# Gate and up products of a Strassen-style feed-forward: the second product of the next weight matrix moved between the third and fourth of the current one

## Chip, core and metric

The kernel runs on one core of one Trainium2 chip. The metric is device time in microseconds (us) for one execution; a version's time is the median of its runs. One execution per version is also recorded by the hardware profiler, with its own time; the trace comes from that execution.

## The reference

A two-layer encoder on a sequence of 1024 rows of width 1024. Layer 0 mixes with FNet and convolution heads, layer 1 with pooling; the change touches neither. Each layer ends with a feed-forward block, whose inner width is 2816, and the change is in the first half of it:

```python
def swiglu_ffn(h, w_gate, w_up, w_down):
    return (jax.nn.silu(h @ w_gate) * (h @ w_up)) @ w_down

for layer in range(DEPTH):
    ...
    h = rmsnorm(x, norm_ffn_g[layer])
    x = x + swiglu_ffn(h, ffn_w_gate[layer], ffn_w_up[layer], ffn_w_down[layer])
```

## The kernel before, in words

Everything is float32. TensorE gets each operand as a high part and a low remainder (`split`, lines 87 to 89: ScalarE casts, VectorE subtracts), and `mm3` (lines 99 to 104) multiplies in three matmuls: high by high (L101), high by low (L102), low by high (L103). In traces every product therefore has the lines L101 to L103, whoever calls it.

**The unit of work.** The 22 blocks of 128 columns of the gate matrix, and of the up matrix, are taken in pairs, 11 a layer. A pair of blocks of one matrix is multiplied with the two halves of the sequence in a Strassen-Winograd scheme of seven products. One product (`product`, lines 553 to 557) is 4 times 3 = 12 matmuls of 128x128 by 128x512. Two of the seven, A11 B11 and A12 B21, are made for all pairs by `gate_up_first` (lines 608 to 624), which also writes the first to memory (`p1_dram`). The other five are made later, in `gate_up_all` (lines 719 to 737), for one matrix of one pair at a time: here called a unit. A layer has 22 units, alternately gate (`up` false) and up (`up` true); gate units end with a silu on ScalarE, up units with a multiplication on VectorE and a store.

**What a unit needs** is set up by `prep` (lines 626 to 644): the saved first product is loaded into an SBUF tile `p1` and copied by ScalarE into a PSUM bank, the seed (L629, L630); two raw weight tiles of 512 KB are loaded (L595); VectorE forms the differences and sums (L635 to L637, L642), and each of five left operands S2, S1, S3, A22, S4 is cast and split (L88, L89).

**What a unit does** (`gate_up_rest`, lines 690 to 710), in the order of the program: product S2 T2 is added onto the seed (L696, "second product"); ScalarE copies the result into the bank `bd` and into the SBUF tile `u2` (L697, L698); S1 T1 goes into the bank `bc` (L699); S3 T3 is added onto `bd` (L700, "third product"); ScalarE copies `bd` to the SBUF tile `x` (L701), VectorE adds `bc` and `x` (L703); then A22 T4 is added onto the same bank `bd` (L705, "fourth product"), which must wait until L701 has read it; S4 B22 is added onto `bc` (L707), and L709 adds `u2`. `fin` (lines 646 to 652) finishes each of the three outputs (L649 silu, L651 multiplication and store).

**Buffers.** PSUM has eight banks: four under the tag "ps", two under "lnp", two under "acc". Seeds come from "ps"; `bc` and `bd` from "ps" in gate units and from "lnp" in up units (`banks2`, L603 to L606). Tiles `p1`, `s3` and `u2` share one tag of four SBUF buffers ("ln", `small`, L58); split weights share ten ("w": five operands of two units, high and low part side by side in one tile), raw weights three. In the profile's names `p` is `p1`, `s` is `s3`, and `u` is `u2`.

**What sets the order.** The loop writes prep of unit u+1 ahead of the products of unit u. A planner in the framework then orders every engine's queue ahead of time by its own estimate of durations: an instruction whose inputs and buffers are there in the estimate is placed, and of several the one that stands earlier in the program. Buffers of a tag are handed out in the program's order. On the chip each queue then runs strictly in that planned order, each instruction waiting on semaphores for what it needs. Weight and `p1` loads are issued from SyncE's queue (SPq), stores from GpSimd's (POOL). In layer 1 `left_sums` (L675 to L688) and `right_sums` (L664 to L673) add loads, VectorE sums and stores per pair for the down projection.

Of the kernel before, what the change touches and what calls it, by code (L numbers as in the profile page):

```python
# [42 lines left out]
def trunk(ctx: ExitStack, tc: tile.TileContext, xT, vecs, cw, w_in, w_out, fmap, pmap,  # L43
          wg, wu, wd, wdq, wdp, cen_m, pcnt, dft_h, dft_l, seq_h, seq_l, out):
    nc = tc.nc
# [9 lines left out]
    def half(name, dt=F32):  # L55
        return arena.tile([P, TH], dt, tag="half", name=name, bufs=HALF_BUFS)

    def small(name, dt=F32):  # L58
        return arena.tile([P, TH], dt, tag="ln", name=name, bufs=4)

    def bank(tag="ps"):
        return psum.tile([P, TH], F32, tag=tag, name=tag, bufs=4 if tag == "ps" else 2)
# [36 lines left out]
    def mm3(ps, lhs, rhs, start, stop, **kw):  # L99
        (lh, ll), (rh, rl) = lhs, rhs  # L100
        nc.tensor.matmul(ps, lh, rh, start=start, stop=False, **kw)  # L101
        nc.tensor.matmul(ps, lh, rl, start=False, stop=False, **kw)  # L102
        mm = nc.tensor.matmul(ps, ll, rh, start=False, stop=stop, **kw)  # L103
        marks.append((marks[-1][0] + 3 * ps.free_size(), mm))
# [85 lines left out]
    def in_w(m, **kw):  # L190
        return load_w(w_in[m], **kw)
# [207 lines left out]
    def pool_w(*args):  # L399
        behind["at"] = max(behind["at"], marks[-1][0]) + 5500  # L400
        return load_w(*args, eng=nc.gpsimd)
# [20 lines left out]
    for h in range(4):  # L422
        w = in_w(h)
# [25 lines left out]
    def fnet1(cp, h):  # L449
        wcs = []  # L450
        for c in (2 * cp, 2 * cp + 1):
            ps = bank()
            psv = ps.rearrange("p (j n) -> p j n", j=2)
            for j in range(2):
                n = len(PLAN[c])
                for i, (zi, tb) in enumerate(PLAN[c]):
                    o = zi * 256 + j * P
                    rhs = tuple(tt[h // 2][:, h % 2, tb:tb + 2, :].rearrange("p a e -> p (a e)")
                                for tt in (tb_h, tb_l))
                    mm3(psv[:, j, :], (z_h[h][:, o:o + P], z_l[h][:, o:o + P]), rhs, i == 0, i == n - 1)  # L460
            wh, wl = half("wch", F32R), half("wcl", F32R)
            nc.scalar.copy(wh, ps)
            TT(out=wl, in0=ps, in1=wh.bitcast(F32), op=ALU.subtract)
            wcs.append((wh, wl))
        return wcs
# [22 lines left out]
    for i, (cp, h) in enumerate(steps):  # L488
        nxt = fnet1(*steps[i + 1]) if i + 1 < len(steps) else None
# [16 lines left out]
    for mp in range(4):  # L506
        w = pool_w(w_out[mp])
# [40 lines left out]
    def opnd(src, alloc):  # L548
        t = alloc("hl", dt=F32R)
        split(t[:, :TH], t[:, TH:], src)  # L550
        return t

    def product(ps, w, b, start, stop):
        for j in range(4):
            c = j * P
            mm3(ps, (w[:, c:c + P], w[:, TH + c:TH + c + P]), (b[j][:, :TH], b[j][:, TH:]),
                start and j == 0, stop and j == 3, skip_group_check=not start)
# [35 lines left out]
    def raw_w(src):  # L593
        raw = arena.tile([P, 1024], F32, tag="raw", name="raw", bufs=3)
        nc.sync.dma_start(raw, src)  # L595
        return raw[:, :TH], raw[:, TH:]
# [3 lines left out]

    nbank = [0]

    def banks2():  # L603
        nbank[0] += 1
        tag = "ps" if nbank[0] % 2 else "lnp"
        return bank(tag), bank(tag)  # L606

    def gate_up_first(layer, p, bt):

        g = half("g11")  # L610
        for i, wsrc in enumerate((wg, wu)):
            a11, a12 = raw_w(wsrc[layer, 2 * p])
            a11, a12 = opnd(a11, wt), opnd(a12, wt)
            ps = bank(("lnp", "ps")[i])
            product(ps, a11, bt["B11"], True, True)
            s1 = half("s1")
            nc.scalar.copy(s1, ps)
            nc.gpsimd.dma_start(p1_dram[layer][p][i], s1)
            product(ps, a12, bt["B21"], False, True)
            if i == 0:  # L620
                nc.scalar.activation(g, ps, AF.Silu)
            else:
                TT(out=g, in0=ps, in1=g, op=ALU.mult)
        store_b(layer, "B11", p, g)

    def prep(layer, p, wsrc):

        p1, bb = small("p1"), bank()
        nc.sync.dma_start(p1, p1_dram[layer][p][int(wsrc is wu)])  # L629
        nc.scalar.copy(bb, p1)  # L630
        a11, a12 = raw_w(wsrc[layer, 2 * p])
        a21, a22 = raw_w(wsrc[layer, 2 * p + 1])
        w = {"seed": bb}
        s3 = small("s3")
        TT(out=s3, in0=a11, in1=a21, op=ALU.subtract)  # L635
        TT(out=a21, in0=a21, in1=a22, op=ALU.add)
        TT(out=a11, in0=a21, in1=a11, op=ALU.subtract)  # L637
        w["S2"] = opnd(a11, wt)
        w["S1"] = opnd(a21, wt)
        w["S3"] = opnd(s3, wt)  # L640
        w["A22"] = opnd(a22, wt)
        TT(out=a12, in0=a12, in1=a11, op=ALU.subtract)  # L642
        w["S4"] = opnd(a12, wt)
        return w

    def fin(layer, up, dst, src, m, t, tmp=None):

        if not up:
            nc.scalar.activation(dst, src, AF.Silu)  # L649
        else:  # L650
            TT(out=dst, in0=src, in1=dst, op=ALU.mult)  # L651
            store_b(layer, "B%d%d" % (m % 2 + 1, t + 1), m // 2, dst)

    def store_b(layer, name, p, src):
        if layer == 0:
            m, t = 2 * p + int(name[1]) - 1, int(name[2]) - 1
            nc.gpsimd.dma_start(a_dram[0][m][:, HALVES[t]], src)
        elif name != "B12":
            nc.gpsimd.dma_start(b_dram[name][p], src)
# [15 lines left out]
    def left_sums(p):  # L675


        q = [half("q") for _ in range(4)]
        for i in range(4):
            nc.sync.dma_start(q[i], wdq[p, :, i, :])  # L680
        a11, a12, a21, a22 = q
        TT(out=a22, in0=a21, in1=a22, op=ALU.add)
        TT(out=a21, in0=a11, in1=a21, op=ALU.subtract)
        TT(out=a11, in0=a22, in1=a11, op=ALU.subtract)
        TT(out=a12, in0=a12, in1=a11, op=ALU.subtract)
        for name, src in (("S3", a21), ("S2", a11), ("S1", a22), ("S4", a12)):
            nc.gpsimd.dma_start(s_dram[name].rearrange("r (j p c) -> r p j c", j=4, c=P)[:, p],  # L687
                                src.rearrange("r (j c) -> r j c", j=4))  # L688

    def gate_up_rest(layer, p, bt, w, up, g):  # L690


        bb, bc, bd = w["seed"], *banks2()
        m1, m2 = 2 * p, 2 * p + 1
        u2, x = small("u2"), half("x")
        product(bb, w["S2"], bt["T2"], False, True)  # L696
        nc.scalar.copy(bd, bb)  # L697
        nc.scalar.copy(u2, bb)  # L698
        product(bc, w["S1"], bt["T1"], True, True)  # L699
        product(bd, w["S3"], bt["T3"], False, True)  # L700
        nc.scalar.copy(x, bd)  # L701
        c22 = x if up else g["22"]
        TT(out=c22, in0=bc, in1=x, op=ALU.add)  # L703
        fin(layer, up, g["22"], c22, m2, 1)
        product(bd, w["A22"], bt["T4"], False, True)  # L705
        fin(layer, up, g["21"], bd, m2, 0)
        product(bc, w["S4"], bt["B22"], False, True)  # L707
        c12 = u2 if up else g["12"]
        TT(out=c12, in0=bc, in1=u2, op=ALU.add)  # L709
        fin(layer, up, g["12"], c12, m1, 1)  # L710
# [3 lines left out]
    def load_right(name, p):  # L714
        raw = half("rawb") if name == "B11" else spare(("cv", "pr")[p % 2])
        nc.sync.dma_start(raw, b_dram[name][p])
        return opnd(raw, big)

    def gate_up_all(layer, bt):
        seq = [(p, up) for p in range(NF // 2) for up in (False, True)]  # L720
        w = prep(layer, 0, wg)
        g = None
        for i, (p, up) in enumerate(seq):
            nxt = None
            if i + 1 < len(seq):
                q, qup = seq[i + 1]
                nxt = prep(layer, q, wu if qup else wg)
            if not up:
                g = {k: arena.tile([P, TH], F32, tag="cvp", name=f"g{k}", bufs=4) for k in ("22", "21", "12")}
            if layer == 1 and not up:  # L730
                left_sums(p)
            gate_up_rest(layer, p, bt, w, up, g)
            if layer == 1 and up:
                right_sums(p, g)
                if p >= NF // 2 - 4:
                    first_right.extend([load_right("B11", len(first_right) + r) for r in range(2)])
            w = nxt

    def new_b():
        return {k: [] for k in ("B11", "B21", "B22", "T1", "T2", "T3", "T4")}  # L740
# [141 lines left out]
    bt, hf = new_b(), []  # L882
# [91 lines left out]


    gate_up_all(1, b1)

    def out_of(lo, hi, inv):
# [117 lines left out]
```

## Time and profile before

| What | Value |
|---|---|
| Median of three runs | 1733.5 us (1731.33 to 1737.66) |
| The profiled execution | 1727.4 us, of which the trace spans 1725.6 us |
| Mean granted TensorE clock | 0.991 |
| TensorE matmuls busy | 1656.9 us, 96% of the span |
| VectorE, ScalarE, GpSimd busy | 1215.0, 793.9, 349.4 us |
| Chain that ended last | 71% TensorE, 11% VectorE, 8% issue, 6% DMA |
| The 22 units of layer 0, from the first to the last L697 | 465.4 to 760.9 us |
| The 22 units of layer 1, likewise | 1179.7 to 1487.4 us |

"Busy" counts an engine as busy while any of its instructions is open. A matmul row lasts some 0.39 us, but the next one starts about 0.23 us after it, so rows overlap, and their sum is more than the busy time. Some matmul records, a few per cent, are missing from a trace. A bracket at the end of a timeline row tells how long that engine had been idle, and whose end released it.

### The profile page before, as it was taken

Reading aid. Unit: us, or ns where it says so; the run is one execution under the profiler, and the core shown is the slowest. Engines: PE = TensorE matmul, PEld = TensorE weight load, DVE = VectorE, ACT = ScalarE, POOL = GpSimd, SP = SyncE. Lnnn points to the kernel's source line nnn. Section 1 sums busy time; section 2 is a strip of 40 time slices with the busy share of each in tenths; the row PEclk is TensorE's granted clock in tenths of the full one; section 3 lists DMA queues with packets and bytes.
Section 4 is the critical chain, followed back from the end, with each engine's and each line's share of the span. In section 5 each row is a group of like instructions: output and inputs, shape, how many; then the busy total and the mean of one; then the engine's idle time right before and its main releaser. Section 6 shows DMA issues by size and latency. Waiting matters only on the chain.

```text
span 1725.6 us, 21770 instructions
## 1 busy us (share of the span) xinstructions
PE 1656.9 (96%) x7790; PEld 1353.6 (78%) x7790; DVE 1215.0 (70%) x1727; ACT 793.9 (46%) x1283; POOL 349.4 (20%) x400
## 2 busy tenths in 40 slices
PE   6998789999999999999999998999999999999997
PEld 4786777777787787779998886777777778888877
DVE  8699997785455656555558877787767677656666
ACT  5555756474444444433334335454343435354443
POOL 4486764211100000000000001211212121204000
PEclk9999899999999999999999999999999999999999
DMA  5121311445633333346443434655767677886664
GB/s 188 49 98 38 126 70 37 165 165 195 243 113 127 116 124 129 120 131 195 132 137 103 155 102 145 216 176 195 232 220 237 209 239 255 278 276 189 201 194 131
DMA packets 101517, 278.23 MB, mean 161 GB/s; under 512 B 13088, under 2 KB 18464, under 8 KB 101408
## 3 DMA queue, kind: packets, MB, share of 16 engines
q1 hardware_dynamic: 77760, 203.16, 36.5%
q0 software_dynamic: 21344, 70.53, 11.7%
q10 hardware_dynamic: 2304, 3.15, 0.5%
q8 instruction: 61, 1.00, 0.2%
q14 instruction: 48, 0.39, 0.1%
HBM read 209.42 MB, written 67.37 MB: 160 GB/s over the span
## 4 chain that ended last, share of the span: by engine, by line
PE 71%; DVE 11%; issue 8%; DMA 6%; ACT 2%; POOL 1%; SPq 0%; POOLq 0%; DVEq 0%; ACTq 0%
PE ps L101 16%; PE ps L103 16%; PE ps L102 16%; PE lnp L101 7%; PE lnp L103 7%; PE lnp L102 7%; DMA p<-p 3%; DVE acc L315 2%; DVE acc L135 1%; DVE hl L89 1%; DMA xin<-in_xT 1%; DMA bT<-cv 1%; ACT x L701 1%; POOL sS L687 0%; ACT hl L88 0%
## 5 line engine op out<-in xcount | busy, mean ns | idle before, releaser
L101 PE MATMUL ps<-hl 128*128 128x512 f32 x704 | 274.9, 396 | 11.2 <-ACT x L701 8.3
L102 PE MATMUL ps<-hl 128*128 128x512 f32 x704 | 276.6, 393 | 0.0
L103 PE MATMUL ps<-hl 128*128 128x512 f32 x704 | 273.5, 394 | 0.0
L88 ACT CAST hl<-raw 128x512 fp32r<-128x512 f32 x264 | 159.7, 619 | 243.8 <-PE lnp L103 96.3
L89 DVE TENSOR_TENSOR hl<-raw,hl 128x512 fp32r<-128x512 f32 x264 | 179.0, 689 | 118.4 <-ACT hl L88 118.2
L88 ACT CAST wh<-raw 128x1024 fp32r<-128x1024 f32 (+4 forms) x147 | 127.9, 870 | 198.8 <-PE ps L102 88.2
L101 PE MATMUL lnp<-hl 128*128 128x512 f32 x528 | 211.7, 401 | 6.1 <-ACT x L701 5.1
L103 PE MATMUL lnp<-hl 128*128 128x512 f32 x528 | 208.2, 395 | 0.0
L102 PE MATMUL lnp<-hl 128*128 128x512 f32 x528 | 208.0, 394 | 0.0
L89 DVE TENSOR_TENSOR wl<-raw,wh 128x896 fp32r<-128x896 f32 (+4 forms) x135 | 136.3, 1012 | 61.0 <-ACT wh L88 50.3
L101 PEld LDWEIGHTS ps<-hl 128*128 128x128 f32 x704 | 132.2, 188 | 51.3 <-ACT x L701 15.2
L103 PEld LDWEIGHTS ps<-hl 128*128 128x128 f32 x704 | 132.2, 188 | 30.5
L102 PEld LDWEIGHTS ps<-hl 128*128 128x128 f32 x704 | 132.3, 188 | 29.1
L305 POOL TENSOR_TENSOR cvp<-cvp,pr 128x512 f32<-128x512 f32 x96 | 137.6, 1434 | 84.6 <-ACT pr L304 80.3
L101 PEld LDWEIGHTS lnp<-hl 128*128 128x128 f32 x528 | 99.5, 188 | 38.7 <-ACT x L701 12.5
L103 PEld LDWEIGHTS lnp<-hl 128*128 128x128 f32 x528 | 99.5, 188 | 23.0
L102 PEld LDWEIGHTS lnp<-hl 128*128 128x128 f32 x528 | 99.6, 189 | 22.2 <-issue 0.7
L101 PE MATMUL ps<-ahl,wh 128*128 128x504 f32 (+2 forms) x358 | 115.3, 322 | 0.0
L103 PE MATMUL ps<-ahl,wl 128*128 128x504 f32 (+2 forms) x358 | 114.8, 321 | 0.0
L102 PE MATMUL ps<-ahl,wh 128*128 128x504 f32 (+2 forms) x358 | 114.7, 320 | 0.0
L101 PE MATMUL ps<-hl,wh 128*128 128x512 f32 (+1 forms) x308 | 111.8, 363 | 0.0
L103 PE MATMUL ps<-hl,wl 128*128 128x512 f32 (+1 forms) x308 | 111.4, 362 | 0.0
(242 smaller groups left out, 3410.9 us busy)
## 6 DMA issues: line engine op xcount, KB each, us to landing
raw<-in_wg SPq DMA_DIRECT2D x66, 512.0 KB, 4.0
raw<-in_wu SPq DMA_DIRECT2D x66, 512.0 KB, 3.8
raw<-in_wd SPq DMA_DIRECT2D x32, 448.0 KB, 3.4
p<-s POOLq DMA_DIRECT2D x44, 256.0 KB, 3.1
p<-p SPq DMA_DIRECT2D x44, 256.0 KB, 4.7
a<-g POOLq DMA_DIRECT2D x44, 256.0 KB, 2.8
q<-in_wdq SPq DMA_DIRECT2D x44, 256.0 KB, 6.2
sS<-q POOLq DMA_DIRECT2D x44, 256.0 KB, 4.6
```

Of the source, the lines that this page charges most:

```text
L88: nc.scalar.copy(hi, src)
L89: (eng or nc.vector).tensor_tensor(out=lo, in0=src, in1=hi.bitcast(F32), op=ALU.subtract)
L101: nc.tensor.matmul(ps, lh, rh, start=start, stop=False, **kw)
L102: nc.tensor.matmul(ps, lh, rl, start=False, stop=False, **kw)
L103: mm = nc.tensor.matmul(ps, ll, rh, start=False, stop=stop, **kw)
L135: TT(out=acc, in0=acc, in1=sq, op=ALU.add)
L305: nc.gpsimd.tensor_tensor(out=a, in0=a, in1=pr, op=ALU.add)
L315: STT(out=acc, in0=src, scalar=wv, in1=acc, op0=ALU.mult, op1=ALU.add)
L701: nc.scalar.copy(x, bd)
```

## The change

`second` is a new function that holds what opened `gate_up_rest`: it takes the bank `bd` and the tile `u2`, multiplies S2 by T2 onto the seed and makes the two copies. It is called for the first unit of a layer right after that unit's `prep`, so ahead of the second unit's `prep`. For each later unit it is called through `between()` inside the products of the unit before it: behind the third product's copy, sum and `fin`, and ahead of the fourth product. In the last unit of a layer `between()` does nothing. The program's order of products thus goes from S2, S1, S3, A22, S4 of one unit to S1, S3 of this unit, S2 of the next, A22, S4 of this one. The number of instructions of each kind is the same. The bank `bd` and the tile `u2` are asked for, and filled, two products earlier relative to their own unit's S1 than before, and the order in which the four "ln" buffers are asked for changes from p1, s3 of unit u+2 after u2 of unit u to p1, s3 of unit u+2 after u2 of unit u+1. The tag of the banks alternates as before.

```diff
-    def banks2():
-        nbank[0] += 1
-        tag = "ps" if nbank[0] % 2 else "lnp"
-        return bank(tag), bank(tag)
...
-    def gate_up_rest(layer, p, bt, w, up, g):
-
-
-        bb, bc, bd = w["seed"], *banks2()
+    def second(bt, w):
+
+        nbank[0] += 1
+        w["tag"] = "ps" if nbank[0] % 2 else "lnp"
+        w["bd"], w["u2"] = bank(w["tag"]), small("u2")
+        product(w["seed"], w["S2"], bt["T2"], False, True)
+        nc.scalar.copy(w["bd"], w["seed"])
+        nc.scalar.copy(w["u2"], w["seed"])
+
+    def gate_up_rest(layer, p, bt, w, up, g, between):
+
+
+
+        bd, u2, bc = w["bd"], w["u2"], bank(w["tag"])
         m1, m2 = 2 * p, 2 * p + 1
-        u2, x = small("u2"), half("x")
-        product(bb, w["S2"], bt["T2"], False, True)
-        nc.scalar.copy(bd, bb)
-        nc.scalar.copy(u2, bb)
+        x = half("x")
         product(bc, w["S1"], bt["T1"], True, True)
         product(bd, w["S3"], bt["T3"], False, True)
         nc.scalar.copy(x, bd)
         c22 = x if up else g["22"]
         TT(out=c22, in0=bc, in1=x, op=ALU.add)
         fin(layer, up, g["22"], c22, m2, 1)
+        between()
         product(bd, w["A22"], bt["T4"], False, True)
         fin(layer, up, g["21"], bd, m2, 0)
         product(bc, w["S4"], bt["B22"], False, True)
...
         w = prep(layer, 0, wg)
+        second(bt, w)
         g = None
...
-            gate_up_rest(layer, p, bt, w, up, g)
+            gate_up_rest(layer, p, bt, w, up, g, lambda: nxt and second(bt, nxt))
```

## The prediction

> **What bounds the kernel now.** I read the page first: share of each engine, then the costliest groups with the idle time before them.
>
> ```profile
> span 1725.6 us, 21770 instructions
> ...
> PE 1656.9 (96%) x7790; PEld 1353.6 (78%) x7790; DVE 1215.0 (70%) x1727; ACT 793.9 (46%) x1283; POOL 349.4 (20%) x400
> ...
> L101 PE MATMUL ps<-hl 128*128 128x512 f32 x704 | 274.9, 396 | 11.2 <-ACT x L701 8.3
> ...
> L101 PE MATMUL lnp<-hl 128*128 128x512 f32 x528 | 211.7, 401 | 6.1 <-ACT x L701 5.1
> ```
>
> TensorE is the bound, and of the 17.3 us for which it stands idle before these two groups, 13.4 us end with L701, the copy of `bd` into `x` that the fourth product waits for. That is the wait that the change puts other work into. The waits of PE by stage, first for layer 1's units and then for layer 0's (columns: total us, times, longest), say where they lie:
>
> ```profile
> PE ps L101 <- ACT x L701: 7.7, 7, 1.5
> PE lnp L101 <- ACT x L701: 3.9, 3, 2.4
> ```
>
> ```profile
> PE lnp L101 <- ACT x L701: 1.3, 1, 1.3
> PE ps L101 <- ACT x L701: 0.6, 3, 0.2
> ```
>
> Layer 1 has 11.6 us of them, layer 0 only 1.9 us. Why so little, at one wait per unit? The timeline of an up unit in layer 0 shows it:
>
> ```profile
> 569.48 0.40 PE L103 MATMUL lnp<-hl 128*128 128x512 f32 x1
> 569.71 0.40 PE L102 MATMUL ps<-hl 128*128 128x512 f32 x1
> ...
> 570.25 0.58 ACT L701 COPY x<-lnp 128x512 f32<-128x512 f32 x1
> ...
> 570.41 0.40 PE L102 MATMUL ps<-hl 128*128 128x512 f32 x1
> ...
> 570.88 0.50 PE L101 MATMUL lnp<-hl 128*128 128x512 f32 x1
> ```
>
> The last matmul of the third product starts at 569.48, the fourth product at 570.88, and between them run matmuls into a "ps" bank. In an up unit only the next unit's seed is in "ps": the planner has already put four matmuls of the next second product (569.71 to 570.41) into the wait, as many as its estimate of the copy holds. The program's new order asks for all twelve. In layer 1 four are not enough:
>
> ```profile
> 1212.39 0.76 SPq L629 DMA_DIRECT2D p<-p  x1
> ...
> 1218.63 0.59 ACT L630 COPY ps<-p 128x512 f32<-128x512 f32 x1 [5.76 <-DMA p<-p]
> 1219.15 0.58 ACT L701 COPY x<-ps 128x512 f32<-128x512 f32 x1
> ...
> 1219.78 0.50 PE L101 MATMUL ps<-hl 128*128 128x512 f32 x1 [1.37 <-ACT x L701]
> ```
>
> On ScalarE's queue the copy to `x` stands behind the copy of a later unit's seed, L630, which waited 5.76 us for its load; `x` follows it by 0.52 us, and TensorE loses 1.37 us.
>
> **The removed wait, from both sides.** From below: the rows of waits sum to 11.6 + 1.9 = 13.5 us. One of them stays, since the last unit of layer 0 has no next second product:
>
> ```profile
> 767.45 0.50 PE L101 MATMUL lnp<-hl 128*128 128x512 f32 x1 [1.25 <-ACT x L701]
> ```
>
> 13.5 - 1.25 = 12.2 us can go. Do they go wholly? The cover grows by eight matmuls. Their spacing comes from two rows fifteen matmuls apart, with no gap between:
>
> ```profile
> 572.37 0.40 PE L101 MATMUL lnp<-hl 128*128 128x512 f32 x1
> ...
> 575.83 0.40 PE L101 MATMUL lnp<-hl 128*128 128x512 f32 x1
> ```
>
> (575.83 - 572.37)/15 = 0.2307 us. A product is 12 x 0.2307 = 2.77 us, a unit 60 x 0.2307 = 13.84 us, and eight matmuls 1.85 us. Of all waits only the longest, 2.4 us, exceeds 1.85, by 0.5. So they go, even if `x` still stands behind a late seed; the 0.5 goes into the bound.
>
> From above: TensorE's whole loss in the stage, by the period of the units. L697 ends each unit's second product; here are the up units of layer 0, then of layer 1 (eleven each, first and last start):
>
> ```profile
> L697 ACT COPY lnp<-ps x11: 570/570/577, 479.8 to 760.9; 128x512 f32<-128x512 f32 x11
> ```
>
> ```profile
> L697 ACT COPY lnp<-ps x11: 570/570/579, 1195.6 to 1487.4; 128x512 f32<-128x512 f32 x11
> ```
>
> (760.9 - 479.8)/20 = 14.06 us and (1487.4 - 1195.6)/20 = 14.59 us a unit, 0.22 and 0.75 us over 13.84. With 21 units per layer that have a follower: 21 x 0.97 = 20.3 us. Some of the difference of 8 us is this, behind the longest wait:
>
> ```profile
> 1202.75 0.50 PE L101 MATMUL lnp<-hl 128*128 128x512 f32 x1 [2.37 <-ACT x L701]
> ...
> 1203.67 0.63 PE L101 MATMUL lnp<-hl 128*128 128x512 f32 x1
> ...
> 1206.66 0.47 PE L102 MATMUL lnp<-hl 128*128 128x512 f32 x1
> ```
>
> Seven spacings take 2.99 us, 0.43 each, where 7 x 0.2307 = 1.61: after 2.37 us of idling TensorE ran at nearly half speed and lost 1.4 us more. No other wait is followed by this; I count it with the wait that goes: 12.2 + 1.4 = 13.6 us. I stay at this end, as it is made of single rows.
>
> The Trainium skill, "TensorE: Matmul & The Clock Gate", section "What's actually happening", has the clock fall to half after an idle window of about 3.4 us. By that rule a 2.37 us wait costs no speed, and the sum would be 1.4 us smaller; the row shows the fall after a shorter gap, and I go by the row.
>
> **What moves, and what covers it.** The copies `bd` and `u2` of the next unit move with the second product; they are wanted by S3 three products later, 8.3 us, and take some 0.6 us each. At the border of two units S4 is now followed by S1 into a bank that nobody has used for a unit. No instruction is added; POOL's stores keep their place.
>
> The critical thing is what feeds the moved product, the four "ln" buffers. Now the load of `p1` is issued about when `u2` is first written, and the rest of the preparation follows:
>
> ```profile
> 564.31 0.36 SPq L629 DMA_DIRECT2D p<-p  x1
> ...
> 564.60 0.59 ACT L698 COPY u<-ps 128x512 f32<-128x512 f32 x1
> ...
> 565.20 0.69 DVE L635 TENSOR_TENSOR s<-raw 128x512 f32<-128x512 f32 x1 [1.36 <-DMA raw<-in_wu]
> ...
> 568.03 0.69 DVE L89 TENSOR_TENSOR hl<-raw,hl 128x512 fp32r<-128x512 f32 x1
> ```
>
> After the change `p1` and `s3` of unit u+2 come behind `u2` of unit u+1 in the order of hand-out. So their load and L635 can begin when the second product of unit u+1 ends, and the second product of u+2 is wanted four products later: 48 x 0.2307 = 11.07 us (before: nine products, 24.9 us). The weights take 568.03 + 0.69 - 565.20 = 3.5 us from L635 to the split S2. The seed takes 0.3 us to the issue (as far apart as the first two rows are), the landing, and 0.6 us for the copy; landing of `p`, layer 1 and then layer 0 (min/median/max):
>
> ```profile
> DMA to landing us min/median/max: 2.3/5.0/8.6
> ```
>
> ```profile
> DMA to landing us min/median/max: 3.1/4.6/5.3
> ```
>
> Even 8.6 us gives 9.5, inside 11.07. In the steady state I cost the move at nothing; the cover left is 5.2 us at the median, and if it is gone, every us more stops TensorE for one.
>
> At the entry it costs something. Before, the second unit's preparation began ahead of the first unit's second product, in layer 1 at 1176.92 against an end at 1179.66:
>
> ```profile
> 1176.92 0.69 DVE L635 TENSOR_TENSOR s<-raw 128x512 f32<-128x512 f32 x1 [1.02 <-DMA raw<-in_wu]
> ...
> 1179.66 0.57 ACT L697 COPY ps<-ps 128x512 f32<-128x512 f32 x1 [4.49 <-PE ps L103]
> ```
>
> Now it follows it, and the product is wanted only S1 and S3 later, 24 x 0.2307 = 5.5 us. The seed needs 0.3 + 5.0 + 0.6 = 5.9 us in layer 1 and 5.5 in layer 0: 0.4 us lost at the medians, 4.0 at 8.6. I take 0.8 us for both layers, between 0 and 4.
>
> **Sum.** 13.6 - 0.8 = 12.8 us gained; bounds 12.2 - 0.5 - 4 = 7.7 and 20.3. The profiled execution of 1727.4 us would take 1714.6. It lies 6.1 us under the median of 1733.5, which would become 1720.7.
>
> **Rivals.** *The next second product is late (slower).* TensorE runs matmuls in order, so if `p1` or S2 is late, A22 and S4 stand behind it though they are ready. This decides if the buffer handed to `p1` is that of the current unit's `u2`, as strict rotation of four would have it: it is free only after the unit's last use of it. S4's end starts L709 (576.73 below); in an up unit L651 then reads `u2` until 577.99 + 0.69, 1.95 us after; in a gate unit L709 is the last, 0.69 us. Then 1.3 on average + 5.0 + 0.6 = 6.9 us against 5.5: 1.4 us a unit in layer 1, 1.0 in layer 0, 21 x 2.4 = 50 us, less the 12.8: 1733.5 + 37 = 1771. It bites from a landing of 3.6 us on. Against it, by rotation this `p1` would now wait for that same `u2`:
>
> ```profile
> 576.73 0.69 DVE L709 TENSOR_TENSOR u<-lnp,u 128x512 f32<-128x512 f32 x1 [1.43 <-PE lnp L103]
> ...
> 577.99 0.69 DVE L651 TENSOR_TENSOR g<-u,g 128x512 f32<-128x512 f32 x1
> ...
> 578.54 0.37 SPq L629 DMA_DIRECT2D p<-p  x1
> ```
>
> The load starts 0.14 us before L651 ends, so it got another buffer. For it: the hand-out may change with the order. 0.14.
>
> The Trainium skill, same page, section "Step-by-step: what each phase is for", says that matmuls stay in program order. The trace agrees: in the 2.37 us at 1202.75 the rest of the second product, whose inputs were there, did not run either.
>
> *Layer 1 is paced by something else (within the bound).* VectorE carries the sums for the down projection there; of 328 us:
>
> ```profile
> 1168.00:1496.00 328.00, 316.46 (x1349) 252.02 (x1348) 237.24 (x370) 137.86 (x246) 71.77 (x119) 0.99 0.69 228
> ```
>
> 237 us is 72%, the DMA share 0.69: room on average, but if the chain from L635 stretches past 11.07 us in each pair, half of the gain returns as waits of the second product: 1733.5 - 6.4 = 1727.1. 0.13.
>
> *The change doesn't do what it says.* The planner fills the wait already; if its order comes out with as few matmuls there as now, the time is 1733.5. Against it: the moved product now stands ahead of the fourth. 0.13.
>
> **How the numbers follow.** About 0.5% (8.7 us) can be told from no change. The forecast has 0.60, nearly all of it beyond 8.7 us: 0.54 faster, 0.06 within; the two rivals without a clear gain add 0.26 to "within", 0.32. Slower is the first rival, 0.14. The range: from the lowest run less the upper bound, 1731.3 - 20.3 = 1711.0, to no change with the runs' own spread, 1737; it leaves out the slow rival and little else. The forecast's own range is 1711 to 1726.
>
> **What would show it.** Right: no PE idle time ended by L701 but in a layer's last unit; twelve matmuls of a second product between third and fourth; unit periods near 13.9 us in both layers; no spacing of 0.43; L635 and the issue of `p1` right behind the second product's end. Wrong: PE idle time ended by L630, or by L88 and L89 at the head of the second product, or `p1` issued only after L709 or L651.

## The result and the profile after

| | before | after |
|---|---|---|
| Median | 1731.2 us (6 runs) | 1723.3 us (1721.31 to 1726.45, 6 runs) |
| Profiled execution, span | 1727.4, 1725.6 us | 1721.3, 1719.2 us |
| Ratio of the runs | | 0.9949, 95% interval 0.993 to 0.9968 |

The change gains about 8 us, 0.5%. 12.8 us were forecast. (The ratio is taken over the runs of both kernels and is not the quotient of the two medians.) The page of the changed kernel, where L703 is the copy to `x` (L701 before), L705 the sum `c22`, L677 the first of the left sums, L691 the copy to `bd`, L624 and L625 load and copy of the seed, L630 the first preparing sum:

```profile
span 1719.2 us, 21624 instructions
...
L101 PE MATMUL ps<-hl 128*128 128x512 f32 x704 | 278.5, 396 | 11.4 <-DVE g L705 4.3
...
L101 PE MATMUL lnp<-hl 128*128 128x512 f32 x528 | 209.7, 397 | 1.6 <-ACT x L703 0.9
```

The waits for `x` no longer lead, but another name stands in the "ps" row: `c22` on VectorE. The waits of PE during layer 1's units (total us, times, longest):

```profile
PE ps L101 <- DVE g L705: 4.3, 5, 1.3
PE ps L101 <- ACT x L703: 1.2, 2, 0.9
PE ps L103 <- DVE hl L89: 1.1, 1, 1.1
PE ps L101 <- ACT hl L88: 1.0, 1, 1.0
PE ps L101 <- ACT ps L691: 0.7, 1, 0.7
PE lnp L101 <- ACT x L703: 0.2, 1, 0.2
```

`x` has gone from 11.6 to 1.4 us; 7.1 us of others came. The order of products is as announced, here in an up unit of layer 0:

```profile
625.10 0.39 PE L103 MATMUL lnp<-hl 128*128 128x512 f32 x1
625.32 0.40 PE L101 MATMUL ps<-hl 128*128 128x512 f32 x1
...
627.89 0.39 PE L103 MATMUL ps<-hl 128*128 128x512 f32 x1
628.12 0.39 PE L101 MATMUL lnp<-hl 128*128 128x512 f32 x1
```

Twelve matmuls into the next unit's seed (625.32 to 627.89), no gap on either side. Layer 0 runs almost without loss, as forecast (its waits sum to 1.7 us, all in its first units and its last one); layer 1, against the forecast of 13.9 us a unit, doesn't: the copies to `x` of the up units, first in layer 0 and then in layer 1, are

```profile
L703 ACT COPY x<-lnp x11: 586/588/588, 486.7 to 764.3; 128x512 f32<-128x512 f32 x11
```

```profile
L703 ACT COPY x<-lnp x11: 562/587/587, 1197.9 to 1486.2; 128x512 f32<-128x512 f32 x11
```

(764.3 - 486.7)/20 = 13.88 us a unit, down from 14.06 and close to the 13.84 of back-to-back matmuls; (1486.2 - 1197.9)/20 = 14.41, down from 14.59 only. The half-speed spacings of 0.43 us are gone.

What took the time in layer 1 is on VectorE and SyncE. In seven of the eleven pairs VectorE stands 3.2 to 5.0 us at L677 until `q` has landed. Here is the fifth pair, first VectorE and then SyncE:

```profile
1291.69 0.69 DVE L677 TENSOR_TENSOR q<-q 128x512 f32<-128x512 f32 x1 [4.32 <-DMA q<-in_wdq]
...
1301.33 0.68 DVE L705 TENSOR_TENSOR g<-ps,x 128x512 f32<-128x512 f32 x1
```

```profile
1282.68 1.83 SPq L675 DMA_DIRECT2D q<-in_wdq  x4
```

The loads of `q` for the left sums are issued at 1282.68, and VectorE is ready for L677 at 1287.4; it stands 4.32 us until `q` has landed at 1291.7. Behind it fifteen more sums and splits run without a gap, and only then `c22`. `x` was there at 1297.81 + 0.58, `c22` starts 2.9 us later, and S4, which adds onto the same bank, waits:

```profile
1302.06 0.50 PE L101 MATMUL ps<-hl 128*128 128x512 f32 x1 [0.56 <-DVE g L705]
```

Before, the same pair's loads were issued at 1287.1 and L682 (the old L677) ran at 1297.4, 10 us after it, with no wait. VectorE's waits for `q` over all eleven pairs, before and after (total us, times):

```profile
  DMA q<-in_wdq: 2.2, 1
```

```profile
  DMA q<-in_wdq: 28.5, 9
```

The wait for `q` is not the whole of it. In the last two pairs L677 hardly waits (0.22 us in all), and yet 4.7 of TensorE's 8.5 us fall there. VectorE had stood before, at the split of `rawb`, an operand that the down projection loads ahead of time in the last four pairs (`load_right`); the waits at these splits, 5.8 and 4.7 us here, are not there in the kernel before. Timeline of VectorE, then of TensorE:

```profile
1434.32 0.69 DVE L89 TENSOR_TENSOR hl<-rawb,hl 128x512 fp32r<-128x512 f32 x1 [5.81 <-ACT hl L88]
```

```profile
1447.53 0.50 PE L101 MATMUL ps<-hl 128*128 128x512 f32 x1 [1.30 <-DVE g L705]
```

### The profile page after: what moved, and what is told of

Read it like the earlier page. It is cut to its first block, busy times and chain, and to the rows that moved or that the text cites. A ratio compares the mean times of both kernels' runs of the same rounds, so it can differ in the third digit from the quotient of the medians.

```text
span 1719.2 us, 21624 instructions
## 1 busy us (share of the span) xinstructions
PE 1653.8 (96%) x7790; PEld 1354.0 (79%) x7790; DVE 1207.3 (70%) x1727; ACT 787.0 (46%) x1283; POOL 351.7 (20%) x400
## 4 chain that ended last, share of the span: by engine, by line
PE 66%; DVE 13%; issue 9%; DMA 8%; POOL 2%; ACT 1%; SPq 1%; POOLq 0%; DVEq 0%; ACTq 0%
PE ps L101 15%; PE ps L102 15%; PE ps L103 15%; PE lnp L101 7%; PE lnp L102 7%; PE lnp L103 7%; DMA p<-p 4%; DVE acc L315 2%; DVE hl L89 2%; DMA q<-in_wdq 1%; DMA xin<-in_xT 1%; DVE acc L135 1%; POOL sS L682 1%; ACT hl L88 1%; POOL bT L654 1%
## 5 line engine op out<-in xcount | busy, mean ns | idle before, releaser
L89 DVE TENSOR_TENSOR hl<-raw,hl 128x512 fp32r<-128x512 f32 x264 | 176.4, 686 | 82.6 <-ACT hl L88 82.3
L88 ACT CAST wh<-raw 128x1024 fp32r<-128x1024 f32 (+4 forms) x147 | 127.9, 871 | 187.7 <-PE ps L102 82.7
L88 ACT CAST hl<-raw 128x512 fp32r<-128x512 f32 x264 | 157.1, 619 | 90.2 <-DVE raw L632 23.7
L89 DVE TENSOR_TENSOR wl<-raw,wh 128x896 fp32r<-128x896 f32 (+4 forms) x135 | 135.9, 1010 | 57.5 <-ACT wh L88 55.2
L101 PEld LDWEIGHTS lnp<-hl 128*128 128x128 f32 x528 | 99.1, 188 | 28.9 <-ACT s L612 4.0
```

Of the source, the lines that this page charges most:

```text
L88: nc.scalar.copy(hi, src)
L89: (eng or nc.vector).tensor_tensor(out=lo, in0=src, in1=hi.bitcast(F32), op=ALU.subtract)
```

## Experiments

Twelve kernels ran, in three groups of four; a group shares a chip and its runs of the kernel before (1726.65, 1730.54 and 1732.17 us), so ratios (time over that of the kernel before in the same group, with a 95% interval) are what compares across groups. The name in brackets is that of the kernel in the table at the end of this section. The theory at first: the wait for `x` is covered, and VectorE's wait for `q` took its place. The rivals: the moved product is fed too late, because `p1` and `s3` are now handed out behind the next `u2`; or VectorE has too much to do.

**Left sums moved to layer 0, with the change (new_left0) and without it (old_left0).** In `gate_up_all`:

```diff
-            if layer == 1 and not up:
+            if layer == 0 and not up:
                 left_sums(p)
```

> The changed kernel with the left sums of the down projection (loads of q, four VectorE sums, stores) made during the units of layer 0 instead of layer 1; nothing is left out. Theory (VectorE's queue stands behind L677 until q has landed, 25 us in layer 1, and holds back the sum c22, the splits and with them TensorE): layer 1's 8.5 us of TensorE waits on L705, L703, L89, L88 and L691 fall under 2 us and its units come down from 14.4 to about 13.9 us each, 8 to 10 us less there; layer 0 may pay up to 4 us for the sums; in all 4 to 10 us under the changed kernel. Rival A (the moved product is fed too late, because p1 and s3 are handed out only after the next u2): layer 1 keeps at least 5 us of its waits, whatever the sums do. Rival B (VectorE has too much to do in layer 1 altogether): the waits halve.

Measured 0.9939 (0.9917 to 0.9961). In layer 1 TensorE waits 2.3 us instead of 8.5:

```profile
PE ps L101 <- DVE g L705: 1.0, 1, 1.0
PE ps L101 <- ACT ps L691: 0.7, 1, 0.7
PE lnp L101 <- ACT x L703: 0.6, 1, 0.6
```

But in layer 0 TensorE now waits 8.0 us, mostly for `x`, and L677 waits 30.4 us for `q` there; the gain of 4 to 10 us on the change did not come. So in the changed order the sums hurt in whichever layer they run. That VectorE merely has too much to do does not explain it: it is busy for 64% of layer 0's units with the sums and for 69% of layer 1's without them. Rival A is not settled by this run.

> The kernel before with the left sums made during the units of layer 0 instead of layer 1; nothing is left out. Theory: the copy to x stands behind the seed copy, and the seed's load is late in layer 1 (median 5.0 us against 4.6) because of the loads of q on the same queue and DMA engines; without them TensorE's waits on L701 in layer 1 fall from 11.6 us to 3 to 6 us, the kernel gains 5 to 8 us, and the change on top of it is worth another 4 to 8 us. Rival: the waits on L701 stay near 11 us, since the seed is late by itself, and the gain is under 2 us.

Measured 1.0086 (1.0059 to 1.0113): the waits on L701 in layer 1 fall from 11.6 to 1.9 us, more than I expected, but layer 0 now has 22.1 us of them. Without the change too the sums disturb the layer that has them, though there VectorE does not wait for `q` at all, so by another way. The expected gain was wrong; the change on top of it is worth 1.5%.

**Only the product moved (new_product_only).** The bank, `u2` and the copies stay at the head of their own unit:

```diff
-        w["bd"], w["u2"] = bank(w["tag"]), small("u2")
         product(w["seed"], w["S2"], bt["T2"], False, True)
-        nc.scalar.copy(w["bd"], w["seed"])
-        nc.scalar.copy(w["u2"], w["seed"])
...
+        u2, x = small("u2"), half("x")
+        nc.scalar.copy(bd, w["seed"])
+        nc.scalar.copy(u2, w["seed"])
```

> The changed kernel, but only the twelve matmuls of the second product are moved; the bank bd, the tile u2 and the two copies stay at the head of their own unit, so that p1 and s3 are handed out as in the kernel before. Theory (q's load): the cover of the copy to x is the same, the waits on L705 behind q stay, and the time is within 3 us of the changed kernel. Rival A (late feeding by the order of hand-out): layer 1's new waits vanish, 5 us or more under the changed kernel.

Measured 0.9884 (0.9863 to 0.9905), 1706.8 us: 20 us gained, and my theory fell in the form I had. With the sums of `q` still in layer 1, TensorE waits there for nothing but the last `x`:

```profile
PE lnp L101 <- ACT x L702: 0.3, 1, 0.3
```

L677's wait for `q` is 2.8 us in all, 2.1 of it in the first pair, against 28.5:

```profile
  DMA q<-in_wdq: 2.8, 4
```

The planner still runs the copies within a microsecond of the moved product's end; what differs is the place of `u2` in the order of hand-out, behind `p1` and `s3` of unit u+2 instead of ahead of them.

**Loads of `q` one unit earlier (new_q_ahead).**

```diff
+            if layer == 1 and up and p + 1 < NF // 2:
+                qn = load_q(p + 1)
```

> The changed kernel with the loads of q issued one unit earlier (in the up unit of the pair before), the sums where they are. Theory (q's load): L677's wait for q falls from 25 us to under 6, the waits of TensorE on L705, L88, L89 in layer 1 from 8.5 us to under 4, and the kernel gains 3 to 7 us. Rivals A and B: no gain beyond 2 us. The six half buffers that q and x share could undo it: then x waits on q's stores and the kernel is slower.

A miss: 0.9982 (0.9966 to 0.9998), no gain on the change and rather a loss, though the two intervals just touch. VectorE's wait for `q` grew to 53.3 us: the planner moved the sums forward along with their loads.

**The change repeated, and `u2` taken out of the order in two ways.** First the changed kernel itself (new_again).

> The changed kernel itself, beside the next three on one chip: 0.993 to 0.997 of the kernel before.

0.9956 (0.9943 to 0.997). Then four shared buffers as two pools of two (new_u2_apart):

```diff
     def small(name, dt=F32):
-        return arena.tile([P, TH], dt, tag="ln", name=name, bufs=4)
+        tag = "l2" if name in ("u2", "lnb") else "ln"
+        return arena.tile([P, TH], dt, tag=tag, name=name, bufs=2)
```

> The changed kernel with the four buffers that p1, s3 and u2 share split in two pools of two: one for u2 (and lnb of the convolution), one for p1 and s3, so that p1 and s3 of unit u+2 no longer come behind u2 of unit u+1. Bank, tile and copies stay with the moved product. Theory (the order of hand-out puts off the preparation, so that VectorE comes to the sums of q before q has landed): L677's wait for q falls from 28 us to under 5, TensorE's waits in layer 1 from 8.5 to under 2 us, about 0.989 of the kernel before. Rival (the early copies to bd and u2, or the early bank, are what hurts): it stays at 0.993 to 0.997. With two buffers only, p1 could wait for s3's end instead; then the seed is late and TensorE waits on L625 or L691.

0.9881 (0.9865 to 0.9896). And with `bd` and its copy moved along, only `u2` and its copy left at the head of its unit (new_bd_early; `u2, x = small("u2"), half("x")` and `nc.scalar.copy(u2, w["seed"])` in `gate_up_rest`):

> The changed kernel with bank bd and its copy moved along with the product, but u2 taken and copied at the head of its own unit, as in the kernel before. Theory (u2's place in the hand-out): p1 and s3 come as early as before, waits as with the product alone, about 0.989 of the kernel before. Rival (early bank and copy hurt): 0.993 to 0.997.

0.9873 (0.9854 to 0.9892), and one wait of TensorE is left in layer 1's units:

```profile
PE lnp L101 <- ACT x L703: 1.0, 1, 1.0
```

Both come out as the order of hand-out has it: neither the early bank nor the early copies cost anything that can be measured, `u2`'s place costs the change some 14 us (1724.0 against 1710.3 and 1708.9).

**Left sums behind the gate unit's products** (new_left_after; the call of `left_sums` moved below `gate_up_rest`).

> The changed kernel with the left sums called behind the gate unit's products instead of ahead of them, so that the planner puts them lower; nothing else moves. Theory (L677 blocks VectorE's queue because it stands ahead of its load): if they come later in VectorE's queue than their load lands, L677's wait falls from 28 us to under 10 and the kernel gains 3 to 10 us on the changed one. If the planner moves the loads of q back as well, the wait stays near 28 us and the time within 2 us.

Another miss, 1.0026 (1.0014 to 1.0038). The loads of `q` moved back too, and VectorE waits longer:

```profile
DVE q L677 <- DMA q<-in_wdq: 58.7, 10, 8.4
```

The issue at 1239.0, say, has VectorE standing at L677 from 1243.9 on; with the loads one unit earlier it was 1238.3 and 1243.1, in the change 1282.7 and 1287.4. In these three kernels VectorE is sent to the sum some 5 us after the issue, whatever the program's order, and the sum can start only later: 9.0 us after the issue in the change, 11.2 and 11.7 in the other two.

**Controls on the kernel before.** The split pools alone, order of products as before (old_u2_apart; same edit as in new_u2_apart):

> The kernel before, its order of products kept, with the four shared buffers split as in new_u2_apart (two for u2 and lnb, two for p1 and s3). A control: if the split by itself were worth the gain of new_u2_apart, it would show here. Theory (the moved product makes the gain, the split only keeps its feeding early): within 0.5% of the kernel before, L701's waits in layer 1 stay at 8 us or more. Rival (early p1 and s3 make the gain, whatever the order of products): 0.985 to 0.991.

0.9897 (0.9883 to 0.9912): the rival was right. Without moving any product, the waits for `x` in layer 1 go from 11.6 us to that of the last unit:

```profile
PE lnp L102 <- ACT x L702: 1.7, 1, 1.7
```

Then the seed's load and copy at the end of `prep` (old_seed_last):

> The kernel before with the load of p1 and the copy of the seed at the end of prep instead of its head; order of products unchanged. Theory: x comes late in layer 1 because it stands behind the copy of a seed whose load has not landed; if the planner now puts that copy behind x, TensorE's waits on L701 in layer 1 fall from 11.6 us to under 4, and the kernel gains 6 to 12 us without the change. If the copy still stands ahead of x, no gain, or a loss of some us as the load is later. Rival (x is late for other reasons, casts that wait for VectorE): the waits stay though the seed has moved.

0.9978 (0.9964 to 0.9991). In 16 of the last 18 units of layer 1 the planner still puts the copy 0.5 to 1.3 us ahead of `x`, so this says little; L701's waits there stay, 13.5 us.

**Half of the second product between** (new_half; six matmuls; the other six and the copies at the head of the next unit):

> new_product_only with half of the second product (six of twelve matmuls) between third and fourth, and the other half with the copies at the head of the next unit. Theory A (the gain is cover: four matmuls before, twelve now): six matmuls cover 0.5 us more than four, L702's waits in layer 1 stay above 5 us and the gain is half of new_product_only's or less (0.992 to 0.998). Theory B (the gain is that the new order leaves the seed's copy no longer ahead of x on ScalarE, so that x is on time): nearly the whole gain, 0.987 to 0.991.

0.9941 (0.9925 to 0.9958), half of new_product_only's gain; L703's waits in layer 1 are 4.5 us, a little under what I set for theory A. Here `p1` is issued no earlier than before (table below), and two matmuls more of cover than the planner had put there give half the gain. So cover is worth something where `x` is late. The time lies in theory A's range, the waits do not.

**Three shared buffers instead of four** (new_ln3), the prediction's slow rival:

> The changed kernel with three shared buffers instead of four, so that p1 or s3 of unit u+2 must wait until the current unit's u2 is free: the slow rival of the prediction, made true. By the prediction's working up to 1.4 us a unit in layer 1 and 1.0 in layer 0, waits of TensorE on L625 or on S2's casts and splits, 1.01 to 1.03 of the kernel before. If the feeding had slack enough (theory of the forecast's steady state), within 0.5% of the changed kernel.

1.0091 (1.0071 to 1.0111), 1.4% above the change. TensorE now waits for the split S2 and its cast, as the rival had it:

```profile
PE ps L103 <- DVE hl L89: 10.8, 11, 1.6
PE ps L101 <- ACT hl L88: 10.6, 8, 2.4
```

**What sets the fastest four apart** is how early `p1` is issued. Here is one unit of layer 1, first before and then in the change, from the issue of `p1` to the copy that ends the unit's second product:

```profile
1286.62 0.38 SPq L629 DMA_DIRECT2D p<-p  x1
...
1315.05 0.57 ACT L697 COPY lnp<-ps 128x512 f32<-128x512 f32 x1 [0.24 <-PE ps L103]
```

```profile
1284.56 0.52 SPq L624 DMA_DIRECT2D p<-p  x1
...
1302.58 0.58 ACT L691 COPY lnp<-ps 128x512 f32<-128x512 f32 x1
```

That is 28.4 us before and 18.0 in the change, whose next unit has 14.1. From the traces, over the last 18 units of layer 1: this time (median), and the time from the seed's copy to the next copy to `x` on ScalarE's queue:

| kernel | issue of `p1` to end of second product | seed's copy ahead of next `x` | left sums wait for `q` | ratio |
|---|---|---|---|---|
| new_q_ahead | 14.7 us | 3.1 to 6.2 us | 53.3 us | 0.9982 |
| new_left_after | 15.1 | 2.7 to 6.7 | 58.7 | 1.0026 |
| new_ln3 | 15.2 | 5.9 to 7.3 | 23.1 | 1.0091 |
| the change | 16.2 | 3.1 to 6.6 | 28.5 | 0.9949 |
| before | 28.5 | 0.5 to 1.3 | 2.2 | 1 |
| old_seed_last | 28.7 | 0.5 to 1.3 in 16 of 18 | none | 0.9978 |
| new_half | 28.9 | 1.0 to 3.7 | 2.8 | 0.9941 |
| new_bd_early | 31.2 | 6.4 to 10.5 | 1.7 | 0.9873 |
| new_u2_apart | 32.3 | 6.4 to 10.1 | 2.0 | 0.9881 |
| new_product_only | 34.1 | 5.8 to 8.9 | 2.8 | 0.9884 |
| old_u2_apart | 40.5 | 4.6 to 9.1 | 1.6 | 0.9897 |

The table has neither the change repeated (new_again, 16.8 us) nor the two kernels with the left sums in layer 0, whose layer 1 has no `q` to wait for. The ratio does not follow the first column row by row: the change is faster than the kernel before with less lead. But only the four kernels with 31 us and more run nearly without loss, in both orders of products. Before, the seed's copy stands right ahead of `x` and its load has just not landed. In the changed order with 16 us the seed is in time, but the preparation comes so late that VectorE meets the sums of `q` before `q`, and at the end of the layer the splits of `rawb` before `rawb`.

## Why the prediction was right in sign and range, and wrong in its sum

- **The wait and its cover: right, but not the only thing at work.** Twelve matmuls stand where four stood, and the waits for `x` went from 13.5 to 2.1 us in both layers. Part of this is not cover: in the change the seed's copy stands 3.1 to 6.6 us ahead of `x` instead of 0.5 to 1.3, and in seven of the ten up units of layer 1 with a follower `x` starts 0.4 us behind the start of the third product's last matmul, as early as in any kernel. In six gate units it starts 1.7 to 3.4 us behind it, and there the cover takes all but 1.2 us in two of them.
- **The size of what could be won: taken from the wrong end.** I took 13.6 us, made of single rows, over the 20.3 us from the periods. Where nothing holds the moved product's feeding back, 20 us are won (new_product_only): the periods had it right. The traces show what the brackets miss. A bracket begins where the row before is taken to end, 0.39 us after its start, though the next matmul could start after 0.23; the row behind a wait follows after 0.33; and gaps as short as that from 570.41 to 570.88, in the prediction's rows, have no bracket at all. Summed over all spacings above 0.26 us in the units of both layers, what exceeds 0.2307 us is 23.3 us before, 16.8 in the change and 2.6 in new_product_only. The differences, 6.5 and 20.7 us, are those of the spans, 6.4 and 20.7. The 1.4 us at half speed need not come in every execution (last section).
- **"In the steady state I cost the move at nothing": the step that failed.** The lead was worked out well: 24.9 us before and 11.07 after, plus a product of 2.77, make 27.7 and 13.8 us; measured are 28.5 and 16.2. And it did suffice for `p1`: TensorE waits for the seed's copy in no unit of layer 1. But I asked only if the seed and S2 would be there in time, and not what else stands in VectorE's queue when the preparation begins 12 us later. There it ran into the sums of `q`, and in the last pairs into the splits of `rawb`; both wait for a load, and `c22` and the splits of S2 came after them. TensorE's new waits, 7.1 us, are named in the profile above, and with `u2` out of the order they are gone but for 0.7 us at the entry (new_bd_early, new_u2_apart). The term put at nothing measures 14 us: the change spans 1719.2 us, new_product_only 1704.9.
- **The entry: inside its bounds, mostly another cause.** 0.8 us forecast, between 0 and 4; measured 1.7, two waits of 0.7 on L691 (the third product right behind the first second product, on the bank that is still being copied) and one of 0.3 on the seed.
- **The rivals.** "Layer 1 is paced by something else" was nearest: about half of the gain returned as waits, though mostly of S4 on `c22` and only in part of the second product (2.1 us on L88 and L89). The slow rival's mechanism is real, as new_ln3 shows, but four buffers keep it away. Its price was worked out too high: 37 us over no change; three buffers cost some 15 over no change (1.0091).
- **The explanation of the wait for `x`.** That it stood behind a late seed is as the trace said. That moving a product is the cure was only argued: old_u2_apart gets 0.9897 by letting `p1` be loaded sooner, and the moved product on top of it gives 0.9881, intervals overlapping. So feeding alone is enough to remove the wait; cover can do it too (new_half), but adds nothing that can be told once `p1` is early. The Trainium skill, "Perfetto Trace Analysis", section "Optimization Strategy", says that the same gap repeated on the engine that should be full can mean too few buffers for the next tile; the split pools, with no buffer more, agree as far as the hand-out goes.

In the profiled executions the 6.4 us divide so: layer 0's last L709 and L712 start at 774.6 and 770.8, 3.8 us apart, of which 2.6 are left at the head of layer 1; its last ones at 1499.7 and 1493.2, so 3.9 us were won in layer 1, where 12.6 were forecast. new_product_only reaches that point at 1478.5. The 2.6 us of layer 0, where the same working has 0.3, come mostly from gaps without a bracket. So the total came out inside the range partly by luck: what could be won was put 7 us too low, and what the move costs 14 us too low.

What stays open: how TensorE's waits divide between `q` and `rawb` as causes was not tested by itself. Which of the fifteen instructions ahead of `c22` would have to give way was not tried, nor an order for VectorE's queue written by hand.

## What to carry to other kernels

When a tile is asked for earlier in the program, list every tile that shares its buffers, and work out by how much each of them, and all the work fed by it, comes later; then look at what else stands in those queues at the new time. Before an order of products is changed to cover a wait, ask why the awaited instruction is late: here a load that could be issued 12 us sooner, through nothing but a split of four buffers in two and two, won as much as the moved product did at its best. And set the size of a gain by the period of the loop against its matmuls, not by the sum of named waits.

## What the runs showed of the hardware that I had not expected

A short stall of TensorE can cost more than itself. Behind the 2.37 us wait in the kernel before, seven matmuls started 0.43 us apart instead of 0.23; in new_left_after three waits, of 1.5, 2.1 and 2.9 us (the first with 0.7 and the last with 0.8 more close behind), were each followed by seven or eight such matmuls, 1.4 to 1.6 us more.

```profile
1313.18 0.50 PE L101 MATMUL ps<-hl 128*128 128x512 f32 x1 [2.89 <-ACT ps L625]
...
1315.18 0.63 PE L101 MATMUL ps<-hl 128*128 128x512 f32 x1
...
1317.74 0.63 PE L101 MATMUL ps<-hl 128*128 128x512 f32 x1
```

These are rows of new_left_after: six spacings in 2.56 us, 0.43 each. Other waits of the same length had no such matmuls behind them. The granted clock in the traces tells the two apart. Here are two stretches of 3.4 us, the one with the wait in the kernel before and the one behind it (length, then busy time and instructions of PE, PEld, the weight loads, DVE, ACT and POOL, then the granted clock, the DMA share and GB/s):

```profile
1200.00:1203.40 3.40, 1.03 (x5) 0.56 (x4) 3.30 (x6) 2.40 (x5) 0.00 (x0) 1.00 0.89 284
1203.40:1206.80 3.40, 3.40 (x10) 2.63 (x9) 1.93 (x4) 0.33 (x1) 0.56 (x1) 0.50 0.46 175
```

In each of the fourteen traces all changes of the granted clock lie on one grid of 3.413 us. Between 330 and 1650 us from the start, the clock fell to 0.50 in 21 stretches of these grids, each time for one stretch. In the stretch ahead of each fall TensorE was busy, as the profile counts it, for at most 48% of the time. In the 5371 stretches at full clock that no fall followed it was busy for at least 46%, and in all but four of them for more than 48.5%. So what counts here is not the length of a wait but how much of one stretch of the grid stood idle.

The same kernel can therefore go either way. All these kernels have a wait of 2.8 us ahead of layer 1's first gate and up products (L543 in the kernel before, near 1050 us). In one profiled execution of the change TensorE was busy for 1.66 of the 3.4 us of that stretch, and the clock stayed; in the other (new_again) it was busy for 0.62, and the clock fell:

```profile
1046.90:1050.30 3.40, 1.66 (x6) 1.07 (x7) 2.28 (x4) 2.08 (x3) 0.00 (x0) 1.00 0.59 166
1050.30:1053.70 3.40, 2.68 (x12) 1.88 (x11) 1.81 (x3) 1.24 (x3) 0.21 (x1) 1.00 0.39 142
```

```profile
1045.20:1048.60 3.40, 0.62 (x4) 0.18 (x2) 3.30 (x7) 3.15 (x5) 0.34 (x1) 1.00 0.44 148
1048.60:1052.00 3.40, 3.40 (x6) 2.04 (x7) 1.16 (x2) 0.68 (x1) 0.00 (x0) 0.50 0.67 233
```

The Trainium skill, "TensorE: Matmul & The Clock Gate", section "What's actually happening", has such a window run free of the kernel. The traces agree with that. Its length of 3.4 us is more than these gaps lasted, so a window need not be idle throughout here, and the measurement decides.
